# Opening with the values' projection: one fixed order on three engines, weights split by chunk, the filters' small layers behind the first half

## The chip, the cores and the metric

The kernel runs on one core of a Trainium2 chip. The metric is device time in microseconds, the median of several executions. Beside the times there is one profiled execution, whose trace gives the start and length of each instruction on each engine: TensorE (PE, with its weight loads as PEld), VectorE (DVE), ScalarE (ACT), GpSimd (POOL) and SyncE (SP), which only issues loads.

## The reference

One transformer layer over 1024 latent tokens and 256 context tokens of width 1024. Only its opening matters here:

```python
def rmsnorm(x, g):
    y = xf * lax.rsqrt(jnp.mean(xf * xf, axis=-1, keepdims=True) + RMS_EPS)
    return (y * g.astype(jnp.float32)).astype(x.dtype)

def modulate(h, shift, scale):
    return h * (1 + scale) + shift
...
mod = jax.nn.silu(c) @ w_ada[i] + b_ada[i]
mod_c = jax.nn.silu(c_ctx) @ w_ada[i] + b_ada[i]
...
hc = modulate(rmsnorm(xc, norm1_g[i]), csh1, csc1)
k_c, v_c = jnp.split(hc @ w_in[i][:, NA_WIDTH:3 * NA_WIDTH], 2, axis=-1)
h = modulate(rmsnorm(x, norm1_g[i]), sh1, sc1)
q, k, v, hv, hx1, hx2, gna, ghy = jnp.split(h @ w_in[i], IN_SPLITS, axis=-1)
...
hid = jnp.sin(fr * (z @ w1.astype(f32) + b1.astype(f32)))     # the filters' small layers
hid = jnp.sin(fr * (hid @ w2.astype(f32) + b2.astype(f32)))
h = (hid @ w3.astype(f32)).reshape(L, 2, HY_ORDER, HY_WIDTH)
```

Attention, long convolutions, gates, output projection and the feed-forward network follow.

## The kernel before, in words

A product of float32 matrices is made of three matmuls: each operand is split into a high part (cast to fp32r on ScalarE, `split`, L176) and a low part (the rest, on VectorE, L177), and wl·hTh, wh·hTl and wh·hTh are added up in a PSUM bank.

The kernel opens with the values' projection, v of the 1024 tokens in two halves of 512, then v of the 256 context tokens. `opening` (L680) runs over these three parts and, in each, over eight chunks k of 128 of the 1024 input channels; per chunk it issues three matmuls (L690) for each of four (context: two) groups of 128 tokens. A part's four banks are evicted by ScalarE (L695, tile `vst`) and stored by GpSimd's queue (`vtok`, L696); `vst` has two buffers.

What a chunk needs comes from the generator `hidden` (L271), one step of which is taken ahead of each chunk:

- `normed`: sums of squares (ScalarE, L289), root (L242), reciprocal (VectorE, L244), then the tiles x are scaled, on VectorE (L298) or, for two of the first four, on ScalarE (L296).
- `ada_block(k)`: shift and scale of 128 channels, by eight matmuls with the modulation block k (L229, 1 MB, tile `wada`), a copy to SBUF (tile `msb`, L232, VectorE), two selector matmuls that turn it into columns (L234), and two small VectorE operations (`mod`, L235 and L236).
- `turned(k)`: four transposes of x (L251), into a bank of `psf` (five banks).
- `chunk(k)`: scale and shift (`htmp`; ScalarE L267 on even k, VectorE L264 on odd k), then the split into hTh and hTl.
- every second chunk, the split of a values' weight `wr`, 128 x 1024 for two chunks at once.

The first step of `hidden` also runs the first of two small filter layers (`filter_hidden`, L361: two matmuls L374, five full passes and two half ones on VectorE, a sine on ScalarE); the second layer stands after the first half. Their inputs `mlp` and `feat` are the first two loads on ScalarE's queue; the filters' last weight `fw` is GpSimd's first load. The filters themselves (`filters`, L384) follow the opening, beside the projection of the other columns (L198).

Within an engine, a scheduler sets the order of the instructions by readiness and priority, except that those marked `keep_in_program_order` keep the order of the code among themselves. Before the change, only the block, weight and later x loads on SP, the later squares and the filters' matmuls are marked here. Engines run their rows strictly in order. ScalarE loads a table (ACT_TABLE_LOAD) where the next function isn't in the one that is loaded.

## Time and profile before

| what | value |
|---|---|
| median of 3 runs | 1719.23 us (1716.78 to 1722.03) |
| profiled execution | 1720.83 us, span 1719.0 us |
| instructions in the span | 22621 |
| TensorE busy | 1658.0 us, 96% |
| TensorE weight loads busy | 1312.4 us, 76% |
| VectorE busy | 1234.7 us, 72% |
| ScalarE busy | 687.2 us, 40% |
| mean clock granted to TensorE | 0.99 |
| moved | 274.38 MB, 160 GB/s |

The span runs from the first to the last instruction on the chip; the execution's time also holds what lies around it (1.8 us). A timeline row reads: start in us, length in us, engine (SPq, ACTq: the queue that issues a load), line of the kernel, operation, output <- inputs, shape, count; in brackets how long the engine had been idle before and what ended that. Rows with a count are several instructions merged, their length reaching from the first start to the last end. Matmuls overlap in their pipeline, so their price is the distance between starts, not their length. A row of waits reads: who waited, for whom, us in total, times, longest.

### The profile page before, as it was taken

How to read it: one execution, taken by the hardware profiler on the slowest of the kernel's cores; microseconds unless marked ns; L12 is line 12 of the kernel's file. 1: busy time of each engine (PE TensorE's matmuls, PEld its weight loads, DVE VectorE, ACT ScalarE, POOL GpSimd, SP SyncE). 2: the span in 40 equal slices, each digit the busy share in tenths (PEclk: the TensorE clock that was granted, in tenths of full speed). 3: DMA queues.
4: the chain of work that ended last, by engine and by line, in shares of the span. 5: the costliest groups of instructions: out<-in, count | busy, mean ns of one | idle time of the engine just before them, and what ended most of it. 6: DMA issues, size and time to landing. Idle time of an engine off the chain costs nothing.

```text
span 1719.0 us, 22621 instructions
## 1 busy us (share of the span) xinstructions
PE 1658.0 (96%) x8128; PEld 1312.4 (76%) x8128; DVE 1234.7 (72%) x2096; ACT 687.2 (40%) x1193; POOL 149.8 (9%) x272
## 2 busy tenths in 40 slices
PE   5899999999999999998998999999999999999997
PEld 3677767777777778787886888788888888878886
DVE  3528789879988787657876867867866566479566
ACT  4433323322221213445656325733333333355455
POOL 0011011000100003202200000000100011100000
PEclk9998999999999999999999999999999999999999
DMA  7316665365564536537655623333432322395344
GB/s 294 145 45 192 233 218 177 112 211 180 167 216 135 187 110 232 160 98 211 202 160 200 191 86 140 130 122 130 153 105 93 110 92 103 112 378 181 98 122 154
DMA packets 110310, 274.38 MB, mean 160 GB/s; under 512 B 15471, under 2 KB 24563, under 8 KB 107893
## 3 DMA queue, kind: packets, MB, share of 16 engines
q1 hardware_dynamic: 90152, 211.86, 36.7%
q0 software_dynamic: 19248, 60.60, 10.6%
q8 instruction: 65, 1.06, 0.3%
q10 hardware_dynamic: 797, 0.45, 0.1%
q14 instruction: 48, 0.39, 0.1%
HBM read 205.48 MB, written 67.39 MB: 159 GB/s over the span
## 4 chain that ended last, share of the span: by engine, by line
PE 75%; issue 10%; DVE 7%; DMA 5%; ACT 3%; POOL 0%; SPq 0%; ACTq 0%; POOLq 0%; DVEq 0%
PE in_ps L198 15%; PE x_ps L1230 15%; PE z_ps L1230 7%; PE dx_ps L1399 5%; PE out_ps L1168 4%; PE in_ps L690 3%; PE dz_ps L1399 3%; PE dft_ps L483 3%; PE hy_ps L198 3%; PE y_ps L1230 2%; PE na_ps L198 2%; PE pt_ps L846 2%; PE pt_ps L860 2%; PE dft_ps L485 1%; PE dft_ps L484 1%
## 5 line engine op out<-in xcount | busy, mean ns | idle before, releaser
L198 PE MATMUL in_ps<-hTh,wl 128*128 128x512 f32 x576 | 233.5, 405 | 1.6 <-ACT proj L659 1.6
L198 PE MATMUL in_ps<-hTh,wh 128*128 128x512 f32 x576 | 228.4, 396 | 0.0
L198 PE MATMUL in_ps<-hTl,wh 128*128 128x512 f32 x576 | 228.3, 396 | 0.0
L198 PEld LDWEIGHTS in_ps<-hTh,wl 128*128 128x128 f32 x576 | 109.2, 190 | 29.1 <-issue 4.8
L198 PEld LDWEIGHTS in_ps<-hTh,wh 128*128 128x128 f32 x576 | 109.2, 190 | 23.6
L198 PEld LDWEIGHTS in_ps<-hTl,wh 128*128 128x128 f32 x576 | 109.3, 190 | 23.3 <-issue 1.0
L176 ACT CAST wh<-wr 128x1024 fp32r<-128x1024 f32 (+1 forms) x56 | 51.8, 925 | 134.0 <-PE in_ps L198 112.7
L177 DVE TENSOR_TENSOR wl<-wr,wh 128x1024 fp32r<-128x1024 f32 (+1 forms) x56 | 59.8, 1068 | 56.3 <-ACT wh L176 55.9
L177 DVE TENSOR_TENSOR ol<-ws,oh 128x512 fp32r<-128x512 f32 x88 | 60.4, 689 | 52.4 <-ACT oh L176 52.2
L177 DVE TENSOR_TENSOR ol<-ar,oh 128x512 fp32r<-128x512 f32 x77 | 52.9, 689 | 46.2 <-ACT oh L176 46.2
L176 ACT CAST oh<-ar 128x512 fp32r<-128x512 f32 x77 | 47.9, 622 | 83.1 <-PE dx_ps L1399 33.1
L176 ACT CAST oh<-ws 128x512 fp32r<-128x512 f32 x88 | 54.7, 622 | 58.0 <-PE x_ps L1230 28.4
L1399 PE MATMUL dx_ps<-ol,oh 128*128 128x512 f32 x176 | 68.8, 391 | 1.7 <-DVE ol L177 1.7
L835 ACT ACTIVATE pe<-pe,mx 128x640 f32<-128x640 f32 x64 | 52.6, 822 | 41.9 <-DVE mx L834 41.9
L1399 PE MATMUL dx_ps<-oh,ol 128*128 128x512 f32 x176 | 67.5, 391 | 1.5 <-DVE ol L177 1.5
L1399 PE MATMUL dx_ps<-oh 128*128 128x512 f32 x176 | 68.6, 390 | 0.0
L483 PE MATMUL dft_ps<-a,matf 128*128 128x512 f32 x128 | 66.3, 600 | 1.9 <-issue 0.9
L834 DVE CUSTOM_DVE_ANT_0 pe<-s_ps,bias 128x640 f32<-128x640 f32 x64 | 50.2, 821 | 20.4 <-PE s_ps L829 20.3
L176 ACT CAST oh<-wr 128x512 fp32r<-128x512 f32 x70 | 43.3, 621 | 52.8 <-PE x_ps L1230 16.0
L177 DVE TENSOR_TENSOR ol<-wr,oh 128x512 fp32r<-128x512 f32 x70 | 48.1, 689 | 22.2 <-ACT oh L176 22.0
L1170 DVE TENSOR_TENSOR x<-x,out_ps 128x512 f32<-128x512 f32 x64 | 42.3, 683 | 13.9 <-PE out_ps L1168 13.9
L1168 PE MATMUL out_ps<-wouh,ml 128*128 128x512 f32 x128 | 50.0, 391 | 0.0
(408 smaller groups left out, 4325.4 us busy)
## 6 DMA issues: line engine op xcount, KB each, us to landing
wr<-in_w SPq DMA_DIRECT2D x52, 512.0 KB, 3.4
ar<-g SPq DMA_DIRECT2D x77, 256.0 KB, 2.9
wr<-in_w_in SPq DMA_DIRECT2D x36, 512.0 KB, 4.5
wal<-in_w_ada SPq DMA_DIRECT2D x64, 256.0 KB, 3.7
...
```

The lines of the kernel that those rows point to most:

```text
L176: self.nc.scalar.copy(hi, src)
L177: self.nc.vector.tensor_sub(lo, src, hi.bitcast(F32))
L198: mm = nc.tensor.matmul(ps, ww[:, k * P:(k + 1) * P], xx[:, k, pos:pos + width], start=(i == 0), stop=(i == n - 1))
L483: nc.tensor.matmul(ps, m[:, 0], v.rearrange("p a b -> p (a b)"), start=True, stop=False)
L690: nc.tensor.matmul(banks[j], hh[xx][:, k, j * P:(j + 1) * P], self.wv[k // 2][ww][:, k % 2], start=(k == i == 0), stop=(k == 7 and i == 2))
L834: nc.vector.tensor_tensor_reduce(pe, ps[:, 256:896], bt, -1.0, 3e38, ALU.add, ALU.min, mx[:, 0:1])
L835: nc.scalar.activation(pe, pe, AF.Exp, bias=mx[:, 0:1], scale=-1.0, accum_out=mx[:, 1:2])
L846: pin(nc.tensor.transpose(pt[:, at:at + P], pe[:, c * P:(c + 1) * P], self.ident))
L1168: nc.tensor.matmul(ps, gg[x][:, tk], ww[y][:, sl], start=(i == 0), stop=(i == n - 1))
L1170: nc.vector.tensor_add(x1[:, sl], x1[:, sl], ps)
L1230: mm = nc.tensor.matmul(ps, w[u][:, k * P:(k + 1) * P], x[v][:, k, :], start=(start and k == 0 and i == 0), stop=(stop and k == 3 and i == 2),
L1399: nc.tensor.matmul(ps[j], x[u][:, j * P:(j + 1) * P], w[v], start=(start and i == 0 and c == 0), stop=(stop and i == N - 1 and k == len(re ...
```

## The change

`hidden`, `opening`, `ada_block`, `turned` and `split` mark nearly everything of the opening `keep_in_program_order`, on TensorE, ScalarE, VectorE and SP. `ada_block` is cut in two, `ada_rows_of` (matmuls and the copy `msb`, now on ScalarE) and `ada_cols_of` (selector matmuls and `mod`). In the first half, chunk k's matmuls (now the four token groups' products with hTh first, the four with hTl last) have the selector matmuls of chunk k+1 in their middle, and its modulation matmuls and the transposes of chunk k+2 stand between chunk k-1's matmuls and chunk k's. `htmp` of the first half is always ScalarE's. The weights are split 128 x 512 at a time, one chunk ahead. Three of the first four x tiles are scaled on VectorE, one on ScalarE. A dummy root (`warm`) follows the Silu of the setup. The filters' layers, with their loads, move to chunks 1 and 5 of the second half; `fw` goes to SP's queue behind the x tiles; SP loads modulation block 0 ahead of the first weight. Lines of the changed kernel are some 10 to 35 higher than before.

ScalarE, from the sums of squares to the first high part (`junk` squares, `rstd1s` root). Before:

```order
L289 ACTIVATE junk,ssq_294<-x 128x1024 x4
L176 CAST wh<-wr 128x1024
L242 ACT_TABLE_LOAD
L242 ACTIVATE rstd1s<-ssq_294,eps 128x4
L296 ACTIVATE x<-x,rstd_353 128x1024
L381 ACT_TABLE_LOAD
L381 ACTIVATE feat<-farg 128x1024
L296 ACTIVATE x<-x,rstd_353 128x1024
```

ScalarE at the same place after the change:

```order
L218 ACT_TABLE_LOAD
L218 ACTIVATE warm<-eps 128x1
L300 ACTIVATE junk,ssq_296<-x 128x1024 x4
L251 ACTIVATE rstd1s<-ssq_296,eps 128x4
L307 ACTIVATE x<-x,rstd_339 128x1024
L236 COPY msb<-ada_ps 128x256
L176 CAST wh<-wr 128x512
L349 ACTIVATE htmp<-hT_ps,mod_248 128x512
L176 CAST hTh<-htmp 128x512
```

The root's table is loaded ahead of the squares, the weight's cast stands behind the root, the sine and its table are gone from here, and `msb` has come to this engine.

TensorE, around the second chunk of the first half. Before:

```order
L690 MATMUL in_ps<-wh,hTh 128x512
L229 MATMUL ada_ps<-wada,csp 32x256 x8
L251 MATMUL hT_ps<-ident,x 128x128 x4
L229 MATMUL ada_ps<-wada,csp 32x256
L234 MATMUL ada_ps<-sel,msb 128x2 x2
L229 MATMUL ada_ps<-wada,csp 32x256 x7
L251 MATMUL hT_ps<-ident,x 128x128 x4
L229 MATMUL ada_ps<-wada,csp 32x256
L234 MATMUL ada_ps<-sel,msb 128x2 x2
L229 MATMUL ada_ps<-wada,csp 32x256 x7
L690 MATMUL in_ps<-wh,hTl 128x512
L690 MATMUL in_ps<-wl,hTh 128x512
```

TensorE there after the change, from the middle of one chunk to the middle of the next:

```order
L243 MATMUL ada_ps<-sel,msb 128x2 x2
L721 MATMUL in_ps<-wl,hTh 128x512
L721 MATMUL in_ps<-wh,hTh 128x512
L721 MATMUL in_ps<-wl,hTh 128x512
L721 MATMUL in_ps<-wh,hTh 128x512
L721 MATMUL in_ps<-wh,hTl 128x512 x4
L232 MATMUL ada_ps<-wada,csp 32x256 x8
L260 MATMUL hT_ps<-ident,x 128x128 x4
L721 MATMUL in_ps<-wl,hTh 128x512
L721 MATMUL in_ps<-wh,hTh 128x512
L721 MATMUL in_ps<-wl,hTh 128x512
L721 MATMUL in_ps<-wh,hTh 128x512
```

A group of eight modulation matmuls is no longer cut by another chunk's selectors, and each kind of work comes once per chunk, hTl last.

ScalarE, between the two halves. Before:

```order
L289 ACTIVATE junk,ssq_294<-x 128x1024 x3
L695 COPY vst<-in_ps 128x512
L289 ACTIVATE junk,ssq_294<-x 128x1024
L695 COPY vst<-in_ps 128x512
L242 ACT_TABLE_LOAD
L242 ACTIVATE rstd1bs<-ssq_294,eps 128x4
L381 ACT_TABLE_LOAD
L381 ACTIVATE hid<-farg 128x1024
L695 COPY vst<-in_ps 128x512 x2
L267 ACTIVATE htmp<-hT_ps,mod_246 128x512
L176 CAST hTh<-htmp 128x512
```

ScalarE between the halves after the change:

```order
L300 ACTIVATE junk,ssq_296<-x 128x1024 x4
L251 ACTIVATE rstd1bs<-ssq_296,eps 128x4
L728 COPY vst<-in_ps 128x512 x2
L176 CAST wh<-wr 128x1024
L728 COPY vst<-in_ps 128x512
L278 ACTIVATE htmp<-hT_ps,mod_248 128x512
L728 COPY vst<-in_ps 128x512
L176 CAST hTh<-htmp 128x512 x2
L395 DMA mlp<-in_mlp 128x259
L397 DMA feat<-in_feat 66x1024
```

The second layer's sine and both table loads are gone from here; a projection weight's cast has come in, one eviction stands between `htmp` and its high part, and the filters' loads follow.

The diff:

```diff
...
-    def split(self, hi, lo, src):
-        self.nc.scalar.copy(hi, src)
-        self.nc.vector.tensor_sub(lo, src, hi.bitcast(F32))
+    def split(self, hi, lo, src, pin=lambda i: i):
+        pin(self.nc.scalar.copy(hi, src))
+        pin(self.nc.vector.tensor_sub(lo, src, hi.bitcast(F32)))
     def weights(self, pool, src, n=D, tag="w", pin=False):
...
         nc.sync.dma_start(cc, a["cc"])
         self.cs = pool.tile([P, 16], F32, name="cs")
+        pin = self.tc.keep_in_program_order
         nc.scalar.activation(self.cs, cc.rearrange("p k w -> p (k w)"), AF.Silu)
+        warm = pool.tile([P, 1], F32, name="warm")
+        pin(nc.scalar.activation(warm, self.eps, AF.Sqrt))
...
-    def ada_block(self, pool, psf, w, k, cs, sel):
+    def ada_rows_of(self, pool, psf, w, cs):
         ps = psf.tile([P, 512], F32, tag="f", name="ada_ps")
         for n in range(8):
             j = n % 4
-            nc.tensor.matmul(ps[32 * j:32 * j + 32, 0:256], cs[:, n], w[:, n], start=(n < 4), stop=(n >= 4),
-                             tile_position=(0, 32 * j))
+            self.tc.keep_in_program_order(nc.tensor.matmul(
+                ps[32 * j:32 * j + 32, 0:256], cs[:, n], w[:, n], start=(n < 4), stop=(n >= 4),
+                tile_position=(0, 32 * j)))
         b = pool.tile([P, 256], F32, tag="msb", name="msb", bufs=2)
-        nc.vector.tensor_copy(b, ps[:, 0:256])
+        self.tc.keep_in_program_order(nc.scalar.copy(b, ps[:, 0:256]))
+        return ps, b
+    def ada_cols_of(self, ps, b, k, sel):
+        nc, pin = self.nc, self.tc.keep_in_program_order
         for n in range(2):
-            nc.tensor.matmul(ps[:, 256 + 2 * n:258 + 2 * n], b[:, n * P:(n + 1) * P], sel, start=True, stop=True)
-        nc.vector.tensor_scalar(self.mod1[:, :, 1, k], ps[:, 256:258], self.bcol[:, 0, k:k + 1], None, op0=ALU.add)
-        nc.vector.tensor_scalar(self.mod1[:, :, 0, k], ps[:, 258:260], self.bcol[:, 1, k:k + 1],
-                                self.ng[:, 0, k:k + 1], op0=ALU.add, op1=ALU.mult)
+            pin(nc.tensor.matmul(ps[:, 256 + 2 * n:258 + 2 * n], b[:, n * P:(n + 1) * P], sel, start=True, stop=True))
+        pin(nc.vector.tensor_scalar(self.mod1[:, :, 0, k], ps[:, 258:260], self.bcol[:, 1, k:k + 1],
+                                    self.ng[:, 0, k:k + 1], op0=ALU.add, op1=ALU.mult))
+        pin(nc.vector.tensor_scalar(self.mod1[:, :, 1, k], ps[:, 256:258], self.bcol[:, 0, k:k + 1], None, op0=ALU.add))
     def rstd(self, pool, ssq, n, tag):
         nc = self.nc
...
-    def turned(self, psf, xs, k):
+    def turned(self, psf, xs, k, pin=False):
         pt = psf.tile([P, 512], F32, tag="f", name="hT_ps")
         for j, x in enumerate(xs):
-            self.nc.tensor.transpose(pt[:, j * P:(j + 1) * P], x[:, k * P:(k + 1) * P], self.ident)
+            mm = self.nc.tensor.transpose(pt[:, j * P:(j + 1) * P], x[:, k * P:(k + 1) * P], self.ident)
+            if pin:
+                self.tc.keep_in_program_order(mm)
         return pt
...
             r = self.rstd(pool, ssq[:, j0:j0 + n], n, tag)
             for j in range(n):
                 x = xs[j0 + j]
-                if j % 2 and not j0:
+                if j == 3 and not j0:
                     nc.scalar.activation(x, x, AF.Copy, scale=r[:, j:j + 1])
                 else:
                     nc.vector.tensor_scalar_mul(x, x, r[:, j:j + 1])
         mlp = self.filter_hidden(mp, hid, psf)
-        next(mlp)
         for n in ("ng", "bcol", "cw", "times"):
             nc.scalar.dma_start(getattr(self, n), a[n])
         nc.vector.tensor_scalar(self.bcol[:, 1, :], self.bcol[:, 1, :], 1.0, None, op0=ALU.add)
+        inorder = self.tc.keep_in_program_order
         for j in range(4):
             load(j)
-        blocks, raws = [], {}
-        inorder = self.tc.keep_in_program_order
+        blocks, raws = [], []
         def block(k):
             if k % 2 == 0:
...
             inorder(nc.sync.dma_start(blocks[k].rearrange("p a b -> p (a b)"), a["w_ada1"][k]))
         def weight(i):
-            raws[i] = pool.tile([P, D], F32, tag="x", name="wr", bufs=8)
-            inorder(nc.sync.dma_start(raws[i], a["wv"][i]))
-        for k in range(4):
-            if k % 2 == 0:
-                weight(k // 2)
-            block(k)
-        weight(2)
+            raw = pool.tile([P, D], F32, tag="x", name="wr", bufs=8)
+            inorder(nc.sync.dma_start(raw, a["wv"][i]))
+            raws.extend((raw[:, 0:512], raw[:, 512:D]))
+            wv = [(pool if i else wpool).tile([P, D], F32R, tag=t, name=t, bufs=3 if i else 2) for t in ("wh", "wl")]
+            self.wv.append([t.rearrange("p (a b) -> p a b", a=2) for t in wv])
+        def split_weight(k):
+            self.split(*(t[:, k % 2] for t in self.wv[k // 2]), raws[k], inorder)
+        block(0)
+        weight(0)
+        block(1)
+        block(2)
+        weight(1)
+        block(3)
         normed(0, 4, "rstd1")
-        turns = [self.turned(psf, xs[0:4], 0)]
+        turns = [self.turned(psf, xs[0:4], k, True) for k in range(2)]
+        ada = self.ada_rows_of(pool, psf, blocks[0], cs)
+        self.ada_cols_of(*ada, 0, sel)
+        split_weight(0)
         for k in range(8):
-            self.ada_block(pool, psf, blocks[k], k, cs, sel)
-            if 1 <= k <= 4:
-                block(k + 3)
-                if k == 2:
-                    weight(3)
+            h = pool.tile([P, 512], F32, tag="htmp", name="htmp", bufs=3)
+            inorder(nc.scalar.activation(h, turns[k], AF.Identity, bias=self.mod1[:, 0, 1, k:k + 1],
+                                         scale=self.mod1[:, 0, 0, k:k + 1]))
+            self.split(*(t[:, k, :] for t in hT[0]), h, inorder)
             if k < 7:
-                turns.append(self.turned(psf, xs[0:4], k + 1))
-            self.chunk(pool, turns[k], 4, self.mod1[:, 0], *hT[0], k)
-            if k % 2 == 0:
-                wv = [(pool if k else wpool).tile([P, D], F32R, tag=t, name=t, bufs=3 if k else 2) for t in ("wh", "wl")]
-                self.split(*wv, raws[k // 2])
-                self.wv.append([t.rearrange("p (a b) -> p a b", a=2) for t in wv])
-            if k == 6:
+                ada = self.ada_rows_of(pool, psf, blocks[k + 1], cs)
+                if k < 6:
+                    turns.append(self.turned(psf, xs[0:4], k + 2, True))
+            yield
+            if k < 7:
+                self.ada_cols_of(*ada, k + 1, sel)
+                if 1 <= k + 1 <= 4:
+                    block(k + 4)
+                    if k in (0, 2):
+                        weight(2 + k // 2)
+                split_weight(k + 1)
+            if k == 5:
                 for j in range(4, 10):
                     inorder(load(j))
-                nc.gpsimd.dma_start(w3, a["fw3"])
-            if k < 7:
-                yield
-        normed(4, 4, "rstd1b")
-        next(mlp)
-        yield
+                inorder(nc.sync.dma_start(w3, a["fw3"]))
+            if k == 7:
+                normed(4, 4, "rstd1b")
+            yield
         hT.append([h1.tile([P, 8, 512], F32R, tag=n, name="hT" + n[-1]) for n in ("hTh", "hTl")])
+        turns = [self.turned(psf, xs[4:8], k, True) for k in range(2)]
         for k in range(8):
-            self.chunk(pool, self.turned(psf, xs[4:8], k), 4, self.mod1[:, 0], *hT[1], k)
-            if k == 7:
+            self.chunk(pool, turns[k], 4, self.mod1[:, 0], *hT[1], k)
+            if k < 6:
+                turns.append(self.turned(psf, xs[4:8], k + 2, True))
+            if k == 3:
                 normed(8, 2, "rstd1c")
+            if k in (1, 5):
+                next(mlp)
+            if k == 6:
+                after = [self.turned(psf, xs[8:], k, True) for k in range(2)]
             yield
         for k in range(8):
-            self.chunk(pool, self.turned(psf, xs[8:], k), 2, self.mod1[:, 1], hcT[0], hcT[1], k)
+            self.chunk(pool, after[k], 2, self.mod1[:, 1], hcT[0], hcT[1], k)
+            if k < 6:
+                after.append(self.turned(psf, xs[8:], k + 2, True))
             yield
...
     def filter_hidden(self, pool, hid, psf):
-        nc.scalar.dma_start(m, a["mlp"])
+        self.tc.keep_in_program_order(nc.scalar.dma_start(m, a["mlp"]))
         z = pool.tile([P, T], F32, name="feat")
-        nc.scalar.dma_start(z[0:66], a["feat"])
+        self.tc.keep_in_program_order(nc.scalar.dma_start(z[0:66], a["feat"]))
...
                 for k in range(8):
                     next(between)
                     hh = hT[h] if h < 2 else hcT
-                    for j in range(n):
-                        for i, (xx, ww) in enumerate(((1, 0), (0, 1), (0, 0))):
-                            nc.tensor.matmul(banks[j], hh[xx][:, k, j * P:(j + 1) * P],
-                                             self.wv[k // 2][ww][:, k % 2], start=(k == i == 0),
-                                             stop=(k == 7 and i == 2))
+                    for i, (j, xx, ww) in enumerate([(j, 0, ww) for j in range(n) for ww in (1, 0)] +
+                                                    [(j, 1, 0) for j in range(n)]):
+                        self.tc.keep_in_program_order(nc.tensor.matmul(
+                            banks[j], hh[xx][:, k, j * P:(j + 1) * P], self.wv[k // 2][ww][:, k % 2],
+                            start=(k == xx == 0 and ww == 1), stop=(k == 7 and xx == 1)))
+                        if h == 0 and i == 3:
+                            next(between)
                 for j, pt in enumerate(banks):
                     st = self.stg.tile([P, 4, P], F32, tag="tm", name="vst").rearrange("p a b -> p (a b)")
-                    nc.scalar.copy(st, pt)
+                    ev = nc.scalar.copy(st, pt)
+                    if h == 0:
+                        self.tc.keep_in_program_order(ev)
                     nc.gpsimd.dma_start((self.vd if h < 2 else self.vcd)[(4 * (h % 2) + j) * P:(4 * (h % 2) + j + 1) * P], st)
```

## The prediction

> **What bounds the kernel now.** The page first: TensorE is busy for 96% of the 1719.0 us span, so only its idle time, or time at the low clock, can be won. The chain of waits then shows where it idles: before 126 us. From there on both orders hold the same work, apart from a few swaps up to about 190 us. The sum is therefore made for the opening alone, and everything behind is taken to move with it. Busy time by stage (length, then busy us of TensorE, its weight loads, VectorE, ScalarE, GpSimd, then clock):
>
> ```profile
> core 0: us, PE busy (x) PEld busy (x) DVE busy (x) ACT busy (x) POOL busy (x), PEclk, DMA share, GB/s
> 0.00:26.70 26.70, 9.41 (x32) 4.03 (x32) 11.75 (x21) 16.36 (x21) 1.38 (x7) 1.00 0.86 331
> 26.70:69.70 43.00, 42.19 (x264) 28.99 (x264) 20.51 (x41) 14.12 (x23) 0.56 (x1) 0.96 0.53 203
> 69.70:77.00 7.30, 1.33 (x5) 0.55 (x4) 5.30 (x8) 6.36 (x9) 1.62 (x3) 0.85 0.42 164
> 77.00:125.70 48.70, 45.34 (x199) 35.28 (x201) 15.48 (x27) 18.12 (x35) 2.62 (x4) 0.92 0.09 34
> 125.70:136.20 10.50, 7.66 (x34) 5.39 (x34) 4.51 (x8) 5.71 (x12) 5.55 (x12) 0.84 0.74 229
> ```
>
> TensorE stands idle 17.3 us before the first values' matmul (26.70), 6.0 between the halves, 3.4 in the rest of the opening and 2.8 behind it. The timeline shows what the first matmul waited for:
>
> ```profile
> 11.54 1.06 ACT L289 ACTIVATE junk<-x 128x1024 f32<-128x1024 f32 x1 [0.18 <-DMA x<-in_x]
> ...
> 13.84 1.28 ACT L242 ACT_TABLE_LOAD   x1
> ...
> 15.14 0.30 ACT L242 ACTIVATE rstd1s<-ssq,eps 128x4 f32<-128x4 f32 x1
> ...
> 17.58 1.41 DVE L298 TENSOR_SCALAR x<-x,rstd 128x1024 f32<-128x1024 f32 x2
> ...
> 22.44 0.42 DVE L232 COPY msb<-ada_ps 128x256 f32<-128x256 f32 x1 [3.46 <-PE ada_ps L229]
> ...
> 24.50 0.78 ACT L267 ACTIVATE htmp<-hT_ps,mod 128x512 f32<-128x512 f32 x1 [1.95 <-DVE mod L236]
> 25.31 0.62 ACT L176 CAST hTh<-htmp 128x512 fp32r<-128x512 f32 x1
> ...
> 25.95 0.69 DVE L177 TENSOR_TENSOR hTl<-htmp,hTh 128x512 fp32r<-128x512 f32 x1 [0.42 <-ACT hTh L176]
> ...
> 26.70 0.50 PE L690 MATMUL in_ps<-wh,hTl 128*128 128x512 f32 x1 [2.58 <-DVE hTl L177]
> ```
>
> The last square waits for the fourth tile of x; between it and the square root lie a weight's cast and a table load; VectorE, busy with the filters' layer, scales x 2.1 us after the root; and the matmul waits for the low part (hTl) too.
>
> Prices of the repeated steps on TensorE (starts count: 22 matmuls from 37.91 to 43.04; the last two rows, 8 apart, at the low clock):
>
> ```profile
> 37.91 0.39 PE L690 MATMUL in_ps<-wl,hTh 128*128 128x512 f32 x1
> ...
> 43.04 0.40 PE L690 MATMUL in_ps<-wh,hTh 128*128 128x512 f32 x1
> 43.27 0.50 PE L234 MATMUL ada_ps<-sel,msb 128*128 128x2 f32 x4
> 43.64 0.63 PE L251 MATMUL hT_ps<-ident,x 128*128 128x128 f32 x4
> 44.20 1.07 PE L229 MATMUL ada_ps<-wada,csp 128*32 128x256 f32 x16
> ...
> 77.60 0.63 PE L690 MATMUL in_ps<-wl,hTh 128*128 128x512 f32 x1
> ...
> 81.02 0.63 PE L690 MATMUL in_ps<-wh,hTl 128*128 128x512 f32 x1
> ```
>
> So a matmul takes 5.13/22 = 0.233 us (0.43 at the low clock), the two selector matmuls 0.4, four transposes 0.57, the eight modulation matmuls 1.05.
>
> **The change, part by part.** *Start (gain).* The filters' loads (feat, mlp, fw) leave the front of the queues, and the fourth x now waits for ng, which ScalarE issues first, instead of feat. The rate over the first 70 us in forty slices, the waits of SP's queue, and the landing of cc, which has ng's size:
>
> ```profile
> GB/s 0 214 332 383 405 389 408 431 412 419 442 421 424 370 7 0 0 0 0 243 440 431 389 440 393 400 426 419 314 14 77 311 236 258 26 0 0 0 0 250
> ```
>
> ```profile
> SPq L284 <- DMA feat<-in_feat: 3.4, 1, 3.4
> SPq L314 <- DMA ng<-in_ng: 2.3, 1, 2.3
> ```
>
> ```profile
> DMA to landing us min/median/max: 2.1/2.1/2.1
> ```
>
> Slices are 1.75 us, so the 2.1 MB of x are through by about 8.3. ScalarE's side is longer: four DMA issues (to 2.8, an estimate at 0.5 each), two table loads and two tiny activations to 5.9, then four squares at 1.2 to 10.7. From there: root 0.3 and reciprocal with hops 0.3, to 11.3; three tiles at 0.70 on VectorE (the fourth beside them on ScalarE), to 13.4; five last transposes at the low clock, to 14.5; eight modulation matmuls at the low clock, 2.1, to 16.6. Today the copy msb to the end of hTh is 22.44 to 25.93, 3.5, and hTl is no longer first: first values' matmul at 20.1, which is 6.6 earlier. msb moves to ScalarE, whose copy of that shape costs
>
> ```profile
> 152.17 0.36 ACT L677 COPY projc<-ctx_ps 128x256 f32<-128x256 f32 x1
> ```
>
> against 0.42, so nothing.
>
> Two loads in a row are where a rule speaks against this. In row 15.14 the root follows its load (13.84 + 1.28) after 0.02 us. The Trainium skill (ScalarE: Activation LUTs, What ACT_TABLE_LOAD costs) puts a switch at 1283 ns plus a drain of some 1380 ns; by it the squares would begin about 2.7 us later, the start would win 3.9 and the kernel would end at about 1708. The trace agrees on the load and shows no drain.
>
> *First half (the fixed order).* Per chunk: ScalarE msb 0.36, half a weight 0.62, htmp 0.78, hTh 0.62 = 2.4 us; TensorE 12 x 0.233 + 0.4 + 1.05 + 0.57 = 4.8. TensorE bounds it if the loop closes: selectors 0.9 us into a chunk, then selectors and modulation 0.9, htmp 0.78, hTh 0.62 and hops, about 2.5, until hTh of the next: 3.4 of 4.8. The weights' casts are as long in total and covered by the 2.4 us that ScalarE is free. Left from the first matmul on: 96 x 0.233 = 22.4, 7 x 0.4 = 2.8, 6 x 1.05 = 6.3, 5 x 0.57 = 2.9: 34.4, to 54.5, today 69.7. The eight modulation groups are no longer torn into 1 + 7, and the filters' matmuls are gone from here.
>
> The loads must keep up. Blocks 0 to 3 and two weights make 7.3 MB with x, through by 21 at 410 GB/s. Block 6 waits on SP's queue for group 3 on TensorE (about 29) and is wanted at 42.5. Modulation blocks took
>
> ```profile
> DMA to landing us min/median/max: 7.0/8.7/11.0
> ```
>
> so 2.5 us are left even at the longest.
>
> *Between the halves (a loss against today's 7.3).* The squares are pinned behind hTh of chunk 7 (51.7).
>
> ```profile
> 61.77 1.96 PE L374 MATMUL mlp_ps<-feat,mlp 128*128 128x512 f32 x4
> ...
> 63.76 1.05 ACT L289 ACTIVATE junk<-x 128x1024 f32<-128x1024 f32 x1
> ...
> 66.12 1.06 ACT L289 ACTIVATE junk<-x 128x1024 f32<-128x1024 f32 x1
> ...
> 69.20 0.58 ACT L695 COPY vst<-in_ps 128x512 f32<-128x512 f32 x1
> ...
> 69.47 1.23 DVE L379 SCALAR_TENSOR_TENSOR farg<-fkf,farg 128x1024 f32<-128x1024 f32 x1
> ...
> 71.64 2.74 DVE L298 TENSOR_SCALAR x<-x,rstd1b 128x1024 f32<-128x1024 f32 x4
> ```
>
> Four squares at 1.18 (63.76 to 66.12 is two), root and reciprocal 0.6, no table load, four tiles 2.74, a transpose: 60.1. But ScalarE's fixed row puts the third eviction ahead of htmp, and it waits for the first one's store (evicted at 57.1, stored by about 60.3), which today took
>
> ```profile
> DMA to landing us min/median/max: 3.1/3.1/3.1
> ```
>
> So third eviction to 60.9, htmp 61.7, fourth 62.3, hTh 63.0: second half at 63.1 instead of 77.0, after 8.6 instead of 7.3 us. Nothing queues behind that store but ScalarE's row itself.
>
> *Second half and context.* 96 matmuls 22.4, ten of them at the low clock + 2.0, transposes 5 x 0.57 + 0.6, the filters' two layers moved here 2 x 2.1 = 4.2: 32.1, to 95.2. The filters' VectorE work (per layer some 6 us, five passes of 0.69 to 1.23 and two half ones) and its sine are covered by 4 to 5 us of TensorE's work per chunk; the cover ends if a low part waits behind more than one pass. Then two evictions free the banks, 0.7, 48 matmuls 11.2, six pairs of transposes 1.8: last values' matmul at 108.9, today 125.6. Gain 16.7.
>
> *Behind it (a loss).* The filters' first loads wait for that matmul:
>
> ```profile
> 125.66 0.33 SPq L389 DMA_DIRECT2D rates<-in_rates  x1
> ...
> 130.12 1.28 ACT L398 ACT_TABLE_LOAD   x1 [3.87 <-DMA rates<-in_rates]
> ...
> 133.61 2.62 PE L403 MATMUL filt_ps<-fw,hid 64*128 64x256 f32 x8 [2.84 <-DVE fv L410]
> ```
>
> These 8 us stay. Today 15 projection matmuls fill them, in the new order 7: 8 x 0.233 = 1.9 us are done later. The rest follows as before.
>
> Sum: 16.7 - 1.9 = 14.8 off the profiled execution's 1720.8 (span 1719.0), 1706.0; the runs' median, 1719.2, lies 1.6 lower: 1704.5. I say 1705.
>
> **Rivals.** A, the loads win little at the start (chance 0.14): ng shares the rings with x, and SP waited for it until 9.08:
>
> ```profile
> 1.84 0.36 ACTq L303 DMA_DIRECT2D ng<-in_ng  x1
> ...
> 9.08 0.80 SPq L314 DMA_DIRECT2D wada<-in_w_ada  x2
> ```
>
>  If it lands as late, x's fourth tile is issued near 8 and lands near 11, as now: the first matmul comes 2 to 3 us later, 1707 to 1708. Against: today 390 KB stand ahead of ng. The drain above would give the same time (0.04).
> B, the three fixed rows catch on each other (0.15): a chunk whose loop takes over 4.8 us, or a low part behind a filter's pass, stops TensorE, where today's order let other matmuls pass. At 0.5 us for eight to twelve chunks that is 4 to 6 us: 1709 to 1711.
> C, slower (0.03): SP's blocks come too late. A block that lands later than 13.4 us after its issue stops everything behind it, once for each pair of blocks; with two pairs released late, it decides from some 21 us of landing on, where the longest was 11.
> D, the start is better than the sum (0.05): if TensorE has the full clock from its first transposes, modulation and transposes take half: 1702.
> The Trainium skill (TensorE: Matmul & The Clock Gate, Part 1) lets the clock rise after a free-running 3.4 us window of work; the low stretch from 77.60 to 81.02 agrees, and which of D and the sum comes is by this rule chance. Nothing changes (0.03): only if the later stages wait for something that does not move, and the chain shows none.
>
> **The numbers.** The likeliest case, 1701.5 to 1707, holds 0.56. With A, the drain and B's middle, 1700 to 1711 holds eight in ten. No change is told from 0.3% of 1719 = 5.2 us on: faster 0.93, the same 0.04 (B at its worst), slower 0.03.
>
> **What would show it.** Right: first values' matmul near 20 us, no TensorE idle over 0.5 us until about 54.5, one gap of 7 to 8 us less its transposes, last values' matmul near 109, the filters' wait near 3.5 us. Wrong at the start: the fourth x lands after 10. Wrong in the order: TensorE waiting each chunk for hTh or hTl, or for a block on SP's queue; a low part waiting behind a filter pass at 75 to 90. Wrong altogether: the idle time behind 126 grows by what the opening won.

## The result, and the profile after

The changed kernel takes 1703.82 us (median of 5 runs, 1699.49 to 1710.82) against 1719.23: a ratio of 0.9914, interval 0.9886 to 0.9942. Run again (first experiment) it took 1701.32: 0.9894, 0.9877 to 0.9910. Both intervals lie wholly below 1, so it is faster, by some 15 to 20 us; 1705.0 was forecast.

The profiled execution after was the shortest of its five (1699.49, span 1697.7) and lies 21.3 us below the one of before. The page's first part; TensorE is busy for 97% instead of 96%:

```profile
PE 1646.1 (97%) x8128; PEld 1306.3 (77%) x8128; DVE 1229.6 (72%) x2089; ACT 688.9 (41%) x1206; POOL 149.5 (9%) x271
```

The windows by stage, cut at the same events as those of before (first values' matmul, end of the first half, start of the second, end of the context part, behind it):

```profile
core 0: us, PE busy (x) PEld busy (x) DVE busy (x) ACT busy (x) POOL busy (x), PEclk, DMA share, GB/s
0.00:19.36 19.36, 6.26 (x48) 3.46 (x48) 3.93 (x13) 11.26 (x19) 0.69 (x6) 1.00 0.91 357
19.36:54.30 34.94, 34.85 (x240) 25.02 (x240) 12.55 (x29) 18.71 (x33) 0.00 (x0) 1.00 0.73 285
54.30:62.28 7.98, 3.76 (x13) 2.33 (x12) 4.88 (x8) 6.18 (x13) 2.48 (x4) 0.66 0.29 97
62.28:105.52 43.24, 43.23 (x188) 33.53 (x188) 26.87 (x41) 20.61 (x36) 2.42 (x5) 0.95 0.19 65
105.52:115.70 10.18, 6.42 (x35) 4.16 (x34) 4.30 (x8) 5.92 (x12) 5.52 (x12) 0.96 0.76 249
```

Inside the halves TensorE does not stand: it is busy for 34.85 of 34.94 and 43.23 of 43.24 us. In the first half that is little news, since it was busy for 42.19 of 43.00 us before; in the second half and the context part it was busy for 45.34 of 48.70. The column PEclk reads 1.00 in the first stage of every run, though rows there run at half speed, as the lengths of equal groups of matmuls show further down; for the start the lengths decide. What is left is the start, the 8 us between the halves and the rates' chain behind. The timeline of the start, the rows that answer to those of before:

```profile
9.24 1.06 ACT L300 ACTIVATE junk<-x 128x1024 f32<-128x1024 f32 x1 [0.18 <-DMA x<-in_x]
...
10.42 0.30 ACT L251 ACTIVATE rstd1s<-ssq,eps 128x4 f32<-128x4 f32 x1
...
10.96 2.08 DVE L309 TENSOR_SCALAR x<-x,rstd 128x1024 f32<-128x1024 f32 x3
...
16.31 0.37 ACT L236 COPY msb<-ada_ps 128x256 f32<-128x256 f32 x1 [4.20 <-PE ada_ps L232]
...
18.69 0.62 ACT L176 CAST hTh<-htmp 128x512 fp32r<-128x512 f32 x1
...
19.36 0.50 PE L721 MATMUL in_ps<-wl,hTh 128*128 128x512 f32 x1 [0.43 <-ACT hTh L176]
```

No cast and no table load stands between the last square and the root now, the scaling follows the root by 0.5 us instead of 2.4, and the first matmul waits for the high part alone. A chunk of the first half, on ScalarE:

```profile
26.28 0.78 ACT L349 ACTIVATE htmp<-hT_ps,mod 128x512 f32<-128x512 f32 x1 [1.45 <-DVE mod L246]
...
28.75 0.37 ACT L236 COPY msb<-ada_ps 128x256 f32<-128x256 f32 x1 [1.04 <-PE ada_ps L232]
```

ScalarE waits twice in each chunk (1.45 and 1.04 us) and TensorE never: the loop closes with room. Between the halves it is ScalarE's chain that TensorE waits for, and behind the opening the rates:

```profile
57.48 1.04 PE L260 MATMUL hT_ps<-ident,x 128*128 128x128 f32 x2 [2.99 <-DVE x L309]
...
59.97 0.59 ACT L728 COPY vst<-in_ps 128x512 f32<-128x512 f32 x1 [1.74 <-DMA vtok<-vst]
...
62.28 0.80 PE L721 MATMUL in_ps<-wl,hTh 128*128 128x512 f32 x1 [0.73 <-ACT hTh L176]
...
105.62 0.33 SPq L420 DMA_DIRECT2D rates<-in_rates  x1
...
109.69 1.28 ACT L429 ACT_TABLE_LOAD   x1 [3.22 <-issue]
...
113.17 1.13 PE L434 MATMUL filt_ps<-fw,hid 64*128 64x256 f32 x6 [3.41 <-DVE fv L441]
```

The last row is the mark used below, "the filters' wait": before it ended at 133.61, now at 113.17, 20.4 us earlier. Ahead of it stand 7 projection matmuls now instead of 15, so 8 x 0.233 = 1.9 us of these 20.4 are work that comes behind it; apart from that and a few swaps both kernels hold the same work there.

### The profile page after: what moved, and what is told of

It reads as the page before. It is cut to its first block, busy times and chain, and to the rows that moved or that the text cites. A ratio compares the mean times of both kernels' runs of the same rounds, so it can differ in the third digit from the quotient of the medians.

```text
span 1697.7 us, 22624 instructions
## 1 busy us (share of the span) xinstructions
PE 1646.1 (97%) x8128; PEld 1306.3 (77%) x8128; DVE 1229.6 (72%) x2089; ACT 688.9 (41%) x1206; POOL 149.5 (9%) x271
## 4 chain that ended last, share of the span: by engine, by line
PE 72%; issue 11%; DVE 9%; DMA 5%; ACT 3%; POOL 0%; SPq 0%; ACTq 0%; DVEq 0%; POOLq 0%
PE x_ps L1265 15%; PE in_ps L198 11%; PE z_ps L1265 7%; PE dx_ps L1434 6%; PE out_ps L1203 4%; PE dz_ps L1434 3%; PE in_ps L721 3%; PE dft_ps L514 3%; PE hy_ps L198 3%; PE y_ps L1265 2%; PE na_ps L198 2%; PE pt_ps L881 2%; PE pt_ps L895 2%; PE dft_ps L515 1%; PE dft_ps L516 1%
## 5 line engine op out<-in xcount | busy, mean ns | idle before, releaser
L198 PEld LDWEIGHTS in_ps<-hTh,wh 128*128 128x128 f32 x576 | 108.6, 188 | 24.4 <-issue 0.7
L176 ACT CAST wh<-wr 128x1024 fp32r<-128x1024 f32 (+1 forms) x60 | 52.6, 877 | 132.1 <-PE in_ps L198 113.4
L985 DVE SCALAR_TENSOR_TENSOR aacc<-wal,cs,aacc 128x512 f32<-128x512 f32 x56 | 41.7, 745 | 13.7 <-DMA wal<-in_w_ada 13.0
```

The costliest lines, as they stand in the source:

```text
L176: pin(self.nc.scalar.copy(hi, src))
L198: mm = nc.tensor.matmul(ps, ww[:, k * P:(k + 1) * P], xx[:, k, pos:pos + width], start=(i == 0), stop=(i == n - 1))
L985: nc.vector.scalar_tensor_tensor(acc, w, c, acc, op0=ALU.mult, op1=ALU.add)
```

## The experiments

Runs of this kernel differ by several us with the same work, so an experiment is read twice: by its median, and by the places of the opening in its profile (us from the span's start; the end of a half is that of its last matmul, to some 0.2). Each ratio is to the kernel before as it was timed again in the same session (medians 1719.39 to 1720.87), and comes from all runs of both, so it is not quite the quotient with 1719.23. Before, e and k have 15 projection matmuls ahead of the filters' wait, v3 has none and the others 7, at 0.233 us each.

| run | median, ratio to before | first matmul | first half | gap | second half | filters' wait ends |
|---|---|---|---|---|---|---|
| before | 1719.23 | 26.70 | 42.9 | 7.4 | 32.2 | 133.61 |
| changed | 1703.82, 0.9914 | 19.36 | 34.9 | 8.0 | 30.7 | 113.17 |
| a_repeat | 1701.32, 0.9894 | 19.80 | 34.9 | 8.0 | 30.7 | 113.56 |
| b_filters_first | 1708.53, 0.9938 | 24.61 | 36.7 | 12.0 | 28.3 | 122.04 |
| c_no_pins | 1703.15, 0.9897 | 20.21 | 35.0 | 8.5 | 31.0 | 114.68 |
| d_no_warm | 1705.29, 0.9915 | 22.06 | 35.2 | 7.9 | 31.0 | 116.25 |
| e_filters_late_only | 1731.80, 1.0061 | 21.18 | 45.6 | 7.2 | 42.7 | 143.49 |
| i_cols_at_once | 1703.43, 0.9895 | 21.19 | 35.5 | 8.5 | 30.2 | 116.02 |
| j_whole_low_first | 1703.22, 0.9900 | 20.77 | 36.0 | 7.9 | 30.7 | 115.96 |
| k_first_half_ahead | 1727.10, 1.0040 | 24.41 | 36.7 | 9.4 | 43.0 | 139.62 |
| m_both_halves_ahead | 1709.07, 0.9932 | 24.44 | 36.7 | 9.9 | 30.2 | 121.74 |
| f_msb_vector | 1702.28, 0.9891 | 19.59 | 35.1 | 7.9 | 30.9 | 113.87 |
| v1_squares_early | 1695.48, 0.9852 | 20.59 | 35.6 | 4.6 | 28.5 | 110.08 |
| v3_rates_early | 1696.80, 0.9860 | 19.38 | 35.0 | 4.6 | 30.2 | 106.25 |

**The changed kernel again** (a_repeat).

> The changed kernel once more, unchanged. Its five runs lay between 1699.49 and 1710.82 us, those of the kernel before between 1716.78 and 1722.03, and its profiled execution was the fastest of the five, so the profiles differ by 21.3 us and the medians by 15.4. Theory: the opening is the same in every execution, since its order is fixed (first values' matmul at 19.4 us, second half at 62.3, last values' matmul at 105.5, all within 0.5), the gain behind it is about 20 us, and the 11 us of spread lie in the rest of the kernel, in both kernels alike; median 1700 to 1706. Rival: the fixed order is at the mercy of the loads, and a slow execution has a late start or a late second half: the first values' matmul moves by several us between the two profiles.

The opening is the same to 0.45 us at every mark (19.80, 62.73, wait 113.56), while the span is 1701.5 instead of 1697.7: of 3.8 us between the two profiles 0.4 arose in the opening and 3.4 behind it. From the mark to the span's end it takes 1585.4 us before and 1583.5 to 1588.9 in all the profiles here but the last one told of. Between the two profiles of the changed kernel the 3.4 us can be placed: the second has two more stretches at the low clock, near 286 and 1061 us (PEclk 0.86 instead of 1.00 from 280 to 292, 0.84 instead of 1.00 from 1055 to 1066), which cost about 1.7 us each. Such scatter keeps effects under 2 to 3 us from showing in the medians.

**The filters back in front** (b_filters_first).

```
hidden:  mlp = self.filter_hidden(...)
+        next(mlp)                       # first layer at the start
...      if k == 7: normed(4, 4, ...)
+            next(mlp)                   # second layer between the halves
-            if k in (1, 5): next(mlp)
-   inorder(nc.sync.dma_start(w3, ...))
+   nc.gpsimd.dma_start(w3, ...)
...      # the loads of mlp and feat lose their marks too
```

> The changed kernel with the filters' small layers and their loads put back: the first layer at the start, the second between the halves. Theory: the loads (0.9 MB, some 2.3 us at the 400 GB/s of the start) and the Sin with its table load between the scaling of x and msb (1.28 + 1.0 us) push the first values' matmul from 19.4 to 24 to 26 us; the gap between the halves grows by the table loads (1.3 to 3 us); the second half loses the filters' eight matmuls (2 layers of 1.72 us) and takes 27 instead of 30.6. Sum: 5 to 6.5 lost, 2 lost, 3.4 won: 1707 to 1710 us, 3 to 6 above the changed kernel. Rival: TensorE has the same work in either place and the start is bound by x and the chain behind it, so the layers are hidden there: first values' matmul below 21, the second half 3.4 shorter, the kernel 1 to 3 us faster than the changed one.

The theory's times hold: 1708.5, first matmul at 24.61. The fourth tile of x lands later, and the scaling waits for VectorE's passes of the filter:

```profile
11.67 1.06 ACT L300 ACTIVATE junk<-x 128x1024 f32<-128x1024 f32 x1 [0.20 <-DMA x<-in_x]
...
15.43 1.15 ACT L307 ACTIVATE x<-x,rstd 128x1024 f32<-128x1024 f32 x1 [2.29 <-DVE rstd L253]
...
15.95 2.07 DVE L309 TENSOR_SCALAR x<-x,rstd 128x1024 f32<-128x1024 f32 x3
```

2.4 us are the loads (11.67 against 9.24) and 2.6 the passes (the root begins at 12.85, and VectorE scales 3.1 instead of 0.5 us behind it). The sine of the theory is not in it: it is over by 18.95, and ScalarE then waits 2.60 us for the modulation matmuls. In place the layers cost the start 5.3, the first half 1.8 and the gap 4.1, and save the second half 2.4: 8.9 at the mark.

**No order marks on the three engines** (c_no_pins).

```
-   inorder(nc.scalar.activation(h, turns[k], ...))      # likewise msb, the splits, mod,
+   nc.scalar.activation(h, turns[k], ...)               # the opening's and ada matmuls, vst
```

> The changed kernel without the marks that fix the order of the opening on ScalarE, VectorE and TensorE (the loads keep theirs); the weights are still split by chunk and the filters are still late. Theory: the fixed order is what lets the first half run at TensorE's pace: with the scheduler's order ScalarE casts both halves of the first weight ahead of msb, and the modulation of the next chunk comes late in each chunk, so the first half takes 38 to 43 us (43.0 in the kernel before) instead of 34.9, and the kernel 1707 to 1712 us. Rival: the split by chunk and the late filters carry the gain and the scheduler's order is as good: first half 34 to 36, kernel within 2 us of the changed one.

The theory falls. The first half takes 35.0 us without these marks (the dummy root, the later squares, the filters' first matmuls and the loads keep theirs), and the filters' wait ends 1.1 to 1.5 us later, which the times do not show (1703.15 against 1701.32 beside it). The "one fixed order" is not what closed the loop; something in the way the code is written is.

**No early table load** (d_no_warm).

```
-   pin(nc.scalar.activation(warm, self.eps, AF.Sqrt))
```

> The changed kernel without the tiny root that draws the square root's table load ahead of the squares. Theory: the load (1.28 us) comes back between the last square and the root, while the last square waits for the fourth tile of x anyway (9.24 us), so the first values' matmul comes at 20.6 instead of 19.36 and everything behind it 1.3 later: less than the times can tell (1702 to 1708 us), to be read in the profile. Rival: without the early load the squares begin 1.5 us sooner and the last of them ends no later than before, so the load is paid for: first values' matmul at 19.4 again. By the Trainium skill (ScalarE: Activation LUTs, What ACT_TABLE_LOAD costs) a switch costs some 1380 ns of drain beside the load of 1283 ns; by that rule the first values' matmul would come at 22.

The first matmul comes at 22.06, 2.7 late, as by the rule of the Trainium skill (ScalarE: Activation LUTs, What ACT_TABLE_LOAD costs); but the rows say otherwise.

```profile
10.62 1.28 ACT L250 ACT_TABLE_LOAD   x1
11.91 0.30 ACT L250 ACTIVATE rstd1s<-ssq,eps 128x4 f32<-128x4 f32 x1
...
19.43 1.93 PE L231 MATMUL ada_ps<-wada,csp 128*32 128x256 f32 x16
```

The root follows the load after 0.01 us, no drain, and stands 1.49 later than in the changed kernel: that is the load, and 0.2 from the last tile of x. The other 1.2 us arise on TensorE, most of them in its second block of modulation, which runs at the low clock (1.93 us, where the changed kernel's took 1.07). That is not the table load's doing: in v1_squares_early, whose instructions up to there are those of the changed kernel and whose transposes begin at 11.88 (11.86), the block takes 1.94 too and the first matmul comes at 20.59. By the lengths of the rows, the full clock comes some 4 to 5 us behind the first transposes in some executions (the changed kernel twice, b, c, f, v3) and some 9 to 10 in others (d, i, j, v1), though up to there the changed kernel, v1 and v3 hold the same instructions; it moves the start by about 1.2 us. The Trainium skill (TensorE: Matmul & The Clock Gate, Part 1) says that the activity window is free-running and the number of slow matmuls varies between runs of one kernel; these traces agree, with the 4 to 5 and the 9 to 10 us. Two numbers met by chance here: the 2.7 us, and the 2.66 that the Trainium skill gives in the section on the table load for load and drain together.

**The late filters alone, on the kernel before** (e_filters_late_only).

```
-        next(mlp)        # both calls of before: at the start, behind the first half
+            if k in (1, 5): next(mlp)        # in the second half
-   nc.gpsimd.dma_start(w3, ...)
+   inorder(nc.sync.dma_start(w3, ...))
...      # the loads of mlp and feat get marks too
```

> The kernel before with one part of the change alone: the filters' small layers and their loads go behind the first half; the order of the rest is the scheduler's, as before. Theory: wherever the opening's order comes from, the filters in front cost what putting them back cost the changed kernel, 8.9 us up to the wait of the filters' matmuls (122.04 against 113.17): the first values' matmul comes at 21 to 22 instead of 26.70, the first half is 2 shorter for the four matmuls at 61.77, the second half 3.4 longer; the wait ends at 124 to 129 instead of 133.61 and the kernel takes 1711 to 1716 us. Rival: without the fixed order the late layers land in VectorE's queue ahead of the second half's low parts and give back what the start wins: the wait ends at 132 or later, the kernel takes 1718 to 1721.

The rival, and worse: 1731.8, 11 us slower than before (ratio 1.0061, 1.0049 to 1.0074). The start wins its 5.5 us, but the first half takes 45.6 and the second 42.7:

```profile
73.99:116.70 42.71, 36.76 (x132) 27.67 (x132) 19.35 (x25) 13.60 (x20) 0.54 (x1) 0.82 0.03 10
```

Three waits for low parts lie in it (2.28 us up to 82.13, 1.80 up to 92.01, 1.87 up to 109.46), and behind each the clock is low (PEclk 0.51 from 82.6 to 86.1, from 92.8 to 96.3 and from 109.9 to 113.4; 0.82 in the mean). The first half has one such wait too, 2.72 us up to 62.56. The wait that ends at 109.46, from the timeline:

```profile
104.81 0.69 DVE L376 TENSOR_SCALAR fkf<-farg 128x1024 f32<-128x1024 f32 x1
...
106.26 1.23 DVE L378 SCALAR_TENSOR_TENSOR farg<-fkf,farg 128x1024 f32<-128x1024 f32 x1
107.25 0.78 ACT L267 ACTIVATE htmp<-hT_ps,mod 128x512 f32<-128x512 f32 x1 [9.62 <-PE hT_ps L251]
107.52 1.22 DVE L379 SCALAR_TENSOR_TENSOR farg<-fkf,farg 128x1024 f32<-128x1024 f32 x1
108.71 0.69 DVE L177 TENSOR_TENSOR hTl<-htmp,hTh 128x512 fp32r<-128x512 f32 x1
...
109.46 0.50 PE L690 MATMUL in_ps<-wh,hTl 128*128 128x512 f32 x1 [1.87 <-DVE hTl L177]
```

ScalarE stood 9.6 us until the transposes came, which TensorE makes only at the chunk's own turn; the low part then stands behind a pass that has begun. So the same move wins 8.9 us in the changed kernel and loses 9.9 in the one before, at the filters' wait. It needs another part of the change to pay, and the marks are not it.

**Selector matmuls at once; whole casts and the low part first; msb on VectorE** (i_cols_at_once, j_whole_low_first, f_msb_vector): three more parts put back, one by one.

```
i:  ada = self.ada_rows_of(...); turns.append(self.turned(..., k + 2, True))
+   self.ada_cols_of(*ada, k + 1, sel)          # not four matmuls later
j:  for i, (j, xx, ww) in enumerate(
-       [(j, 0, ww) for j in range(n) for ww in (1, 0)] + [(j, 1, 0) for j in range(n)]):
+       [(j, xx, ww) for j in range(n) for xx, ww in ((1, 0), (0, 1), (0, 0))]):
    def split_weight(k):                        # the whole tile, in every second chunk
f:  -   nc.scalar.copy(b, ps[:, 0:256])
    +   nc.vector.tensor_copy(b, ps[:, 0:256])
```

> The changed kernel with the selector matmuls of a chunk's modulation right behind the eight modulation matmuls and the transposes, instead of four matmuls later. Theory: those four matmuls hide the copy msb (0.37 us and its hops); without them TensorE waits about 0.5 us in each of seven chunks, the first half takes 37 to 39 us instead of 34.0 (first matmul to the last group of four), and the kernel 1704 to 1707 us, 3 to 4 above the changed one run beside it. Rival: the transposes (0.6 us) cover the copy and the modulation is ready earlier: first half 34.0 to 34.5, kernel within 1 us.

> The changed kernel with two parts put back to the form of before: a weight tile is cast whole in every second chunk (1.05 and 1.21 us) instead of half a tile in each (0.62 and 0.68), and each token tile's matmuls begin with the low part. All order marks stay. Theory: ScalarE and VectorE have 2.5 us free in each chunk of 4.82, so the whole casts cost nothing, and the low part is ready (28.43) before its chunk begins (29.03); only the first chunk of each part waits for its low part: first values' matmul at 20.0 instead of 19.36, second half and context part 0.5 to 0.7 late each; first half 34.0, kernel 1 to 2 us above the changed one. Rival: these two carry the first half's gain of some 7 us: TensorE waits in every second chunk, first half 38 or more, kernel 5 to 8 above.

> The changed kernel with the copy msb back on VectorE (0.42 us instead of 0.37). Theory: either engine is free when it comes (ScalarE waits 1.04 us for it in each chunk), so nothing moves: first half 34 to 35 us, kernel 1701 to 1705 us. Rival: on VectorE it stands behind the low part (0.69 us) in each chunk, the modulation comes 0.5 later and TensorE waits: first half 37 or more, kernel 3 above the changed one.

None of them matters by more than a microsecond or two: 1703.4, 1703.2 and 1702.3 us, first halves of 35.5, 36.0 and 35.1. In i a chunk takes 4.96 instead of 4.82 us: the transposes cover the copy, and the theory's 0.5 us of waiting does not come. In j TensorE waits once, 0.81 us, for a low part in the last chunk, and the beginning of its first half ran at the low clock, which is the rest of its 1 us.

**Work ahead in the first half, then in both** (k_first_half_ahead, m_both_halves_ahead), on e, with no marks:

```
k:  turns = [self.turned(psf, xs[0:4], k) for k in range(2)]
    self.ada_block(..., blocks[0], 0, cs, sel)
    for k in range(8):
        self.chunk(pool, turns[k], ...)
        if k < 7: self.ada_block(..., blocks[k + 1], k + 1, cs, sel)
        if k < 6: turns.append(self.turned(psf, xs[0:4], k + 2))
m:  the same with turns = ... xs[4:8] in the second half, xs[8:] in the context part
    if k == 3: normed(8, 2, "rstd1c")          # was k == 7
```

The last line, the scaling of the context tokens four chunks earlier, is part of the change too.

> The kernel before with the filters late (the run that took 1731.8 us, wait of the filters' matmuls ended at 143.49), and one thing more: in the first half the modulation is made one chunk ahead and the transposes two, as in the changed kernel. No order marks on the engines, weights cast whole, low part first. Theory: taking the marks, the half casts, the order of the three products or the place of the selector matmuls out of the changed kernel left its first half at 34 to 36 us, so what is left is the work ahead: the first half falls from 45.6 to 35 to 37 us, the second half stays at 42, the wait ends at 133 to 135 and the kernel takes 1719 to 1723 us. Rival: no one part carries it, and without marks and half casts the first half stays above 40: 1725 us or more.

> The same, with the transposes two chunks ahead in the second half and the context part too. Theory: in the second half TensorE waited for low parts that stood behind the filters' passes on VectorE (1.80 to 2.28 us at a time, and more where the records show it as busy at the low clock); with the transposes ahead, ScalarE and VectorE start a chunk one chunk sooner and the passes are hidden: second half 31 to 33 instead of 42 us, wait at 114 to 118, kernel 1701 to 1705 us, the changed kernel's time without a single mark on the order of the three engines. Rival: the passes (6 us a layer) are longer than a chunk (3.5 us), so without the order marks they still hold low parts back: second half 36 or more, kernel 1708 to 1714.

The windows of k's first half, then of the second half in k and in m:

```profile
24.41:61.10 36.69, 36.17 (x236) 25.78 (x236) 14.40 (x30) 10.66 (x18) 0.67 (x1) 0.95 0.55 215
```

```profile
70.52:113.55 43.03, 37.08 (x132) 27.94 (x132) 19.36 (x25) 13.60 (x20) 0.54 (x1) 0.81 0.03 10
```

```profile
71.08:101.28 30.20, 30.20 (x131) 23.35 (x131) 20.92 (x30) 13.04 (x21) 0.54 (x1) 0.94 0.03 9
```

This is the part, and the second half shows it best: ahead there takes it from 43.0 to 30.2, with the filters' passes still in it, and the time from 1727.1 to 1709.1. Of the 12.8 us, 6.0 are TensorE's waits (37.08 us busy of 43.03, then 30.20 of 30.20) and some 6.4, an estimate from the two lengths and clocks (0.81 and 0.94), the low clock behind them. The context part behind it gains 5 us more (from the second half's end to the last values' matmul 17.7, then 12.5), which may be the transposes or the earlier scaling of its tokens.

Ahead in the first half takes that from 45.6 to 36.7, but it begins 3.2 later and so ends only 5.7 earlier (66.8 and 61.1): TensorE's idle time in it falls by 2.2 us (42.90 busy of 45.62, 36.17 of 36.69), and 24 of its 260 instructions, the modulation, selectors and transposes of one chunk, now stand ahead of the first values' matmul.

Both runs miss their forecast of the whole, each by some 4 us, and land among the times of their rivals, since the first matmul comes at 24.4: there the scheduler puts other work ahead of chunk 0. From m:

```profile
20.44 1.03 ACT L176 CAST wh<-wr 128x1024 fp32r<-128x1024 f32 x1
21.38 0.62 ACT L176 CAST hTh<-htmp 128x512 fp32r<-128x512 f32 x1
...
22.57 1.22 DVE L177 TENSOR_TENSOR wl<-wr,wh 128x1024 fp32r<-128x1024 f32 x1
...
23.70 1.29 DVE L177 TENSOR_TENSOR hTl<-htmp,hTh 128x512 fp32r<-128x512 f32 x2
...
24.44 0.50 PE L699 MATMUL in_ps<-wh,hTl 128*128 128x512 f32 x1 [3.08 <-DVE hTl L177]
```

A whole weight is cast ahead of hTh and of hTl, and the first matmul wants hTl. In c (half casts, low part last, no marks) the first matmul came at 20.21, in j (marks, whole casts, low part first) at 20.77: with the work ahead, marks, or half casts with the low part last, are each enough; with neither it is 24.4 (without the work ahead, e came at 21.18). m ends 8.6 us behind the changed kernel at the mark: 5.1 from the start, 1.8 from the first half, 2.0 from the gap, less 0.5 in the second half.

**Better than both** (v1_squares_early): ScalarE's two waits in each chunk are room for the squares of x's next tiles, and a third store buffer (the squares' output tile, idle by then) spares the 1.74 us.

```
+   if k == 6: square(5)                 # behind hTh of chunk 6
+   if k in (5, 6): square(2 * k - 6)    # x4, x6: behind the weight's cast
-   if k == 7: normed(4, 4, "rstd1b")
+   if k == 7: normed(4, 4, "rstd1b", 3) # only the last square here
-   st = self.stg.tile([P, 4, P], F32, tag="tm", name="vst")...
+   st = xpool.tile([P, D], F32, tag="junk", bufs=1)[:, 0:512] if j == 2 else (as before)
```

> The changed kernel, and more: three of the four squares between the halves (1.18 us each on ScalarE) move into the gaps of 1.0 and 1.4 us that ScalarE has in each chunk of the first half, and the third eviction gets a buffer of its own instead of waiting 1.74 us for the first one's store. Theory: the gap between the halves is ScalarE's chain of squares, root, evictions and htmp, so the second half starts 3 to 4 us earlier, at 58.5 to 59.5 instead of 62.28, and the kernel takes 1697 to 1700 us. Rival: the squares wait for their tiles of x or push msb and htmp back, and each chunk of the first half that holds one grows by 0.5 to 1 us: the second half starts at 61 or later and the time is that of the changed kernel.

1695.48 us: 0.9852 (0.9836 to 0.9868). The windows of the gap and the second half:

```profile
56.20:60.82 4.62, 2.02 (x13) 1.25 (x12) 3.27 (x5) 3.83 (x8) 2.50 (x4) 1.00 0.47 173
60.82:89.36 28.54, 28.54 (x131) 22.14 (x131) 21.79 (x32) 14.15 (x23) 0.27 (x1) 1.00 0.13 42
```

The gap is 3.4 us shorter, as expected; the second half is 2.2 shorter as well, since TensorE keeps the full clock (1.00 instead of 0.66 and 0.92). The first half with the squares in it takes 0.7 more, about what its low clock at the start explains. The time lies 1.5 us below the forecast. What the squares and the buffer win apart was not tested, and the clock is not the gap's doing alone, as the next run shows.

**The rates early too** (v3_rates_early).

```
+   inorder(nc.sync.dma_start(self.rates0, a["rates"][0]...))   # behind fw, into a place of its own
-   rates = pool.tile(...); nc.sync.dma_start(rates, a["rates"][hf]...)
+   rates = self.rates0;  if hf: nc.sync.dma_start(rates, a["rates"][hf]...)
```

> The kernel with the squares early (1695.48 us, wait of the filters' matmuls ended at 110.08), and the filters' first row of rates loaded with their last weights into a place of its own instead of behind the opening. Theory: behind the opening TensorE waits 4.0 us for a chain that starts with this load's issue (105.6 in the changed kernel, where Exp's table load begins at 109.69); with the rates there, the table load follows the last eviction, and the wait falls below 0.7 us: kernel 1691 to 1693 us. Rival: the wait is for the table load, four Exp and a product on VectorE (3.5 us behind the last eviction), so the filters' matmuls still stand 2 to 3 us, and the kernel stays within 1.5 us of 1695.5.

```profile
106.25 1.96 PE L444 MATMUL filt_ps<-fw,hid 64*128 64x256 f32 x8 [2.14 <-DVE fv L451]
```

The rival: the wait falls from 4.0 to 2.1 us only. The filters' wait ends 3.8 earlier than in v1, but 1.8 of that are the seven projection matmuls that stood ahead of it there; 1.9 are the wait, and the last values' matmul comes only 0.2 earlier. The start is 1.2 earlier than in v1, by the clock, and the clock takes it back behind the gap:

```profile
54.40:58.98 4.58, 1.98 (x13) 1.24 (x11) 3.22 (x5) 3.78 (x8) 2.51 (x4) 1.00 0.47 175
58.98:89.16 30.18, 30.18 (x130) 23.27 (x130) 21.78 (x32) 14.14 (x23) 0.27 (x1) 0.94 0.12 40
```

The gap is v1's (4.58 against 4.62, the last wait 1.93 against 1.94), yet here the clock falls behind it and the second half takes 30.2 instead of 28.5. So of the 2.2 us that v1 won in the second half, this trace shows 0.6.

A tile turned near 296 us comes only 0.07 earlier than in v1, and the median, 1696.80, is not below v1's. Behind the filters' wait this profile, the slowest of its five, takes 7.2 us longer than v1's: 1.6 for the seven matmuls and some 5.2 at the low clock in three places (PEclk 0.84 against 0.92 from 270 to 292 us, 0.83 against 1.00 from 770 to 780, 0.89 against 1.00 from 1050 to 1066). Why the clock fell there was not settled.

## Why the prediction was right, point by point

The time (1705.0 for 1703.82 and 1701.32) was right, mostly by its terms. That it came so close to 1703.82 is partly luck: the terms up to the last values' matmul gave 3.4 us too little gain, and the medians of the same kernel lie 2.5 us apart.

- *Start*, 20.1: 19.36 and 19.80, in other executions of the same rows 20.6. b confirms the term: loads and filter layer cost 5.3 of the 7.3. The two loads in a row cost no drain (5.44 - 4.15 - 1.28 = 0.01 us), and the early root is worth 1.3 (the root came 1.5 later in d, 0.2 of it by the last tile of x). Rivals A and the drain are out: the first square began at 5.55 and the last at 9.24. D, the full clock from the first transposes, did not come.
- *First half*, 34.4, to 54.5: 34.94, to 54.3. Right in size, wrong in its heading, "the fixed order". The sum was TensorE's work alone, and it holds, marks or none (c: 35.0), with the modulation one chunk ahead and the transposes two (k). Against before, little of the gain is waiting: TensorE's idle time falls by 0.7 us only. An estimate from the rows for the 8.0 us: 2.0 are the filters' matmuls at 61.77, 1.6 a modulation group and a set of transposes that now come ahead of the first values' matmul (264 instructions then, 240 now), 1.7 the clock (0.96, now 1.00); some 2 us stay open. Rival B, rows that catch on each other, did not come either.
- *Between the halves*, 8.6: 7.98. The chain came as told, with the third eviction behind the first one's store (1.74 us).
- *Second half and context*, 32.1 + 13.7: 30.74 + 12.50. Here terms were mis-sized: four transposes come at 0.44 instead of 0.57 (67.33 to 67.77), a filter layer's matmuls at 1.3 instead of 2.1 (67.77 to 69.08), and the 0.7 for two evictions did not occur: the context part's first matmul starts at 93.02, 0.15 behind the last two transposes. The low clock's 2.0 was right: the first twelve matmuls took 62.28 to 67.33, 5.05 instead of 2.8. The rows behind them:

```profile
67.33 0.60 PE L260 MATMUL hT_ps<-ident,x 128*128 128x128 f32 x4
67.77 1.88 PE L405 MATMUL mlp_ps<-feat,mlp 66*128 66x512 f32 x4
69.08 0.80 PE L721 MATMUL in_ps<-wl,hTh 128*128 128x512 f32 x1
```

 With 0.7 and 0.6 us won at the start and in the gap and 0.5 lost in the first half, the last values' matmul came at 105.5 instead of 108.9, 20.1 earlier than before instead of 16.7. The step's reason, that VectorE's passes "are covered by 4 to 5 us of TensorE's work per chunk", was half a reason: with as much work per chunk, e and k lost 12 us there. The cover is the transposes two chunks ahead.
- *Behind it*, a loss of 1.9: not to be seen. The chain from the last matmul to the wait's end took 7.65 instead of 7.95, and from the mark to the end the two profiles took 1584.5 and 1587.9 where before took 1585.4. The scatter of this stretch, 5 us, is larger than the term; the medians' gain of 15 to 20 us is thus not told apart from the 18.5 that the filters' wait shows without the moved matmuls.
